# PSUM banks around the values of a forgetting attention: scores' banks for the values, sums' banks for the first projections

## The chip, the cores and the metric

The kernel runs on one core of one Trainium2 chip. The metric is device time in microseconds for one execution; lower is better.

## The reference

One layer of a streaming encoder, for 512 tokens of 1024 channels in float32. Of its three sub-layers the first matters here: four token mixers work on the same normalized input `h`, and their outputs are merged by gates.

```python
h = _rms_norm(x, norm_mix_pre[l])
(a_q, a_k, a_v, f_q, f_k, f_v, f_g, c_u, s_x, s_b, s_c) = jnp.split(h @ w_in[l], cuts, axis=-1)
...                       # A: differential attention, 4 heads, chunk-causal: softmax - lam * softmax, times a_v
ya = (_rms_norm(ya, diff_norm[l]) * (1.0 - lambda_init)).reshape(B, S, BR_W)

log_f = jax.nn.log_sigmoid(f_g.astype(jnp.float32) + b_fgt[l].astype(jnp.float32))
yf = _forgetting_attention(f_q..., f_k..., f_v..., log_f, t_pos)   # B: 8 heads, causal, bias from cumsum(log_f)
...                       # C: convolution module, D: short gated convolution
proj = jnp.einsum('bsnc,ncd->bsnd', br, w_branch[l])
gates = jax.nn.sigmoid(h @ w_gate[l] + b_gate[l]).reshape(B, S, N_BRANCH, D)
mixed = jnp.sum(gates * proj, axis=2) @ w_out[l]
x = x + _rms_norm(mixed, norm_mix_post[l])
...                       # 2. cross-attention into memory tokens, 3. gated MLP
```

## The kernel before

Every product is made at close to full float32 precision from three passes. An operand is split into a high part (rounded by ScalarE's copy, L155 for results in PSUM, L190 for weights) and a low part (VectorE's difference, L156 and L191), and `mm3` (L232 inside `matmul`) adds high x high, high x low and low x high in one PSUM bank. Weights come in blocks of 512 KB on SyncE's queue into a ring of two raw buffers (`wr`) and are split into rings of four high and four low tiles (`wh`, `wl`); `run_blocks` fetches three blocks ahead of the body that uses them.

**Banks.** PSUM has eight banks of 128 x 512 float32, and the kernel gives them out as four rings of two: `mm` (projections and gates), `av` (the sums of values weighted by attention), `sc` (scores) and `tr` (transposes). A tile of a ring waits until the tile two before it has been read. `bank()` without a tag takes `mm` and `av` in turn while `turn_of.shared` is set, and `mm` alone otherwise; `share(flag)` sets this.

**Background tasks.** Attention heads and the convolution's normalization are Python generators in a queue `bg`. Each `yield` names a cost and a wait. `bg.tick()` between the matmul blocks steps the first two tasks of the queue as far as their waits and a credit allow; `bg.drain(name)` steps all tasks of that name to their end. So the generators fix the order in which instructions are written. The order in which each engine runs them is laid down by the framework when the kernel is built: it places an instruction once it takes its inputs and buffers to be ready, the one written first ahead of others. So TensorE runs some of the values' matmuls ahead of pieces of a head that were written earlier. On the chip each engine keeps to its order.

**The stretch around the change,** in the order in which it is written (`mixer_jobs`):

- `v_jobs`: values of differential attention, four token tiles in four banks taken in turn (`av`, `mm`, `av`, `mm`), split into tile `v`.
- `share(False)`, then for each differential head h its query and key (`qk_jobs`: 24 matmuls each, `body_q` leaves the bank by L806 and L807, `body_k` by L815 to L817), and 0, 2, 4 and 6 blocks of gate 2 behind heads 0 to 3. `then(qk)` puts the head's task into the queue.
- `a_task`: steps 0 to 3 each do the scores of one query tile (two `sc` banks, left by VectorE at L877) and a softmax that ends at L887. Steps 1 to 4 transpose the tile before (`tr` bank, `pth` and `ptl`). Steps 3 and 5 do the two halves of the values into one `av` bank, which L892 copies to `head_ck`. Then the head is turned from channels to tokens and back: VectorE transpose (L672), a store to DRAM and four loads on GpSimd's queue (L682, L686), a norm (L898 to L903), VectorE transpose (L678), store and loads again, and L911 with a split into `y["a"]`.
- `drain("a")`, then `vf_jobs`: values of the forgetting attention and its forget gates' inputs, 520 columns in two groups (256 and 264), so two banks a token tile. Token tiles 0 and 1 run over the four weight blocks as they come; then, from the same four blocks, which stay held, tiles 2 and 3. One bank of each token tile is an `mm` and one an `av` bank. `done(t)` splits a token tile into the values tile, which shares the buffer `v` with the differential heads' values. `forget_gates` then makes the cumulative log-forget rows, which go to DRAM (`crows`) on GpSimd's queue.
- `kv_blocks(0)`: query and key of the first pair of forgetting heads, then gate 0 and the other pairs. `f_task` loads rows of `crows` into tiles `ck`, which share their two buffers with `head_ck`.

Of the kernel before, what the change touches and what calls it, by code (L numbers as in the profile page):

```python
# [18 lines left out]
F32R = mybir.dt.float32r  # L19
# [6 lines left out]
P = 128  # L26
S = 512
D = 1024
NT = S // P
# [17 lines left out]
class Background:  # L47
# [26 lines left out]
            while self.credit > 0 and task in self.queue and task[2] <= self.clock:  # L74
                self.credit -= self.step(task)

    def drain(self, name):
        while any(t[0] == name for t in self.queue):
            for task in [t for t in self.queue if t[0] == name][:self.width]:
                self.step(task)  # L80

# [2 lines left out]
def hybrid_layer(ctx: ExitStack, tc: tile.TileContext, a: dict, out: bass.AP):  # L84
# [705 lines left out]

    query_ends = {}

    def qk_jobs(cq, ck, j, then):


        st = {}
        rows = (slice(0, HD), slice(HD, P))

        def body_q(hi, lo):
            qk = st["qk"] = m1p.tile([P, 6, S], F32R, tag="qk", name="qk", bufs=2)  # L800
            for c, r in enumerate(rows):
                G.memset(qk[rows[1 - c], 4 + c].bitcast(F32), 0.0)
            ps = bank()
            channel_major(ps, (hi, lo), ht)
            for c, r in enumerate(rows):
                A.copy(qk[r, c], ps[r])  # L806
                low = V.tensor_tensor(qk[rows[1 - c], c], ps[r], qk[r, c].bitcast(F32), ALU.subtract)  # L807
            query_ends[cq, j] = low.ins

        def body_k(hi, lo):  # L810
            qk = st["qk"]
            ps = bank()
            channel_major(ps, (hi, lo), ht)
            for c, r in enumerate(rows):
                A.copy(qk[r, 2 + c], ps[r])  # L815
                A.copy(qk[rows[1 - c], 2 + c], ps[r])
                V.tensor_tensor(qk[r, 4 + c], ps[r], qk[r, 2 + c].bitcast(F32), ALU.subtract)  # L817
            then(qk)

        yield *cols(w_in, cq + j * P), body_q  # L820
        yield *cols(w_in, ck + j * P), body_k
# [31 lines left out]
    def head_tile(tag):  # L853
        return m1p.tile([P, S], F32, tag=tag, name=f"head_{tag}", bufs=2)

    def a_task(h, qk, v):
        es, pt, av = {}, None, None
        for step in range(6):
            if step in (3, 5):
                if av is None:  # L860
                    av = bank("av")
                vh, vl = (x[:, :, h * P:(h + 1) * P] for x in v[0])
                values(av, lambda kt: ((vh[:, kt], 0), (vh[:, kt], 1), (vl[:, kt], 0)), pt, step // 2 - 1)
            cost = 0.0
            if 1 <= step <= 4:
                if step in (1, 3):
                    pt = pt_tiles()
                to_keys_major(es.pop(step - 1)[:, 0], step, pt[0], pt[1], (step - 1) % 2)
                cost += 0.1 + 0.15 * step
            if step < 4:  # L870
                qt, w = step, (step + 1) * P
                e = es[qt] = e4()
                st = m1p.tile([P, 8], F32, tag="st8", name="st8", bufs=4)
                for c in range(2):
                    ps = bank("sc")
                    scores(ps, qk, c, qt * P, w)
                    V.tensor_tensor_reduce(e[:, c, :w], ps[:, :w], mask_a[:, S - w:], scale=1.0,  # L877
                                           scalar=-3.0e38, op0=ALU.add, op1=ALU.max,
                                           accum_out=st[:, c:c + 1])
                V.tensor_scalar(st[:, 2:4], st[:, 0:2], -HD ** -0.5, None, ALU.mult)  # L880
                for c in range(2):
                    A.activation(e[:, c, :w], e[:, c, :w], AF.Exp, bias=st[:, 2 + c:3 + c],
                                 scale=HD ** -0.5, accum_out=st[:, 4 + c:5 + c])
                V.reciprocal(st[:, 6:8], st[:, 4:6])
                V.tensor_scalar(st[:, 7:8], st[:, 7:8], lam, None, ALU.mult)
                A.activation(e[:, 1, :w], e[:, 1, :w], AF.Copy, scale=st[:, 7:8])
                V.scalar_tensor_tensor(e[:, 0, :w], e[:, 0, :w], st[:, 6:7], e[:, 1, :w], ALU.mult,  # L887
                                       ALU.subtract)
                cost += 0.6 + 0.0035 * w
            if step == 5:  # L890
                o = head_tile("ck")
                A.copy(o, av)  # L892
            yield cost, 3.5

        sq = head_tile("fbias")
        x = head_tile("ck")
        yield from turn(x, o, NT, sq, f"head_tok{h}")
        A.activation(sq, x, AF.Square, scale=1.0 / math.sqrt(P))  # L898
        ms = m1p.tile([P, NT], F32, tag="ms4", name="ms4", bufs=2)
        V.tensor_reduce(ms, sq.rearrange("p (a t c) -> p t a c", a=4, t=NT), AX.XY, ALU.add)  # L900
        r = rstd_of(m1p, [ms], NT)
        x4 = x.rearrange("p (a t c) -> p a t c", a=4, t=NT)
        V.tensor_tensor(x4, x4, r.unsqueeze(1).unsqueeze(3).to_broadcast([P, 4, NT, 32]), ALU.mult)  # L903
        yield 1.5, 1.0
        o = head_tile("ck")
        sq = head_tile("fbias")
        yield from turn(o, x, NT, sq, f"head_chan{h}", True)
        if "a" not in y:
            y["a"] = (y8b(), y8b())
        z = head_tile("fbias")  # L910
        A.activation(z.rearrange("p (t b c) -> p t b c", t=NT, b=4), o.rearrange("p (b t c) -> p t b c", b=4, t=NT),  # L911
                     AF.Identity, scale=half["dn"])
        split(z, y["a"][0][:, h], y["a"][1][:, h])
        yield 0.6, 0.0
# [5 lines left out]
    def vf_jobs(dst):  # L920
# [20 lines left out]
        for kb in range(4):  # L941
            def body(hi, lo, kb=kb):
                held.append((hi, lo))
                if kb == 0:
                    dst.append(m1p.tile([P, NT, 8, 2, HD], F32R, tag="v", name="v"))
                    dst.append(small["fz_raw"].rearrange("p (t h) -> p t h", t=NT))
                    ps.update({(t, g): bank(("mm", "av")[g]) for t in range(2) for g in range(2)})
                products(kb, (0, 1))
                if kb < 3:
                    return  # L950
                done(0)
                done(1)
                bg.tick()
                ps.update({(t, g): bank(("mm", "av")[g]) for t in range(2, 4) for g in range(2)})
                for b in range(4):
                    products(b, (2, 3))
                    bg.tick()
# [150 lines left out]
        return None, None, f  # L1108

    def kv_blocks(p):  # L1110
        return qk_jobs(O_FQ, O_FK, p, lambda qk: bg.add(f_task(p, qk, vf), "f"))

    def mixer_jobs():
        yield from c_jobs()
# [17 lines left out]
            yield then(lambda f=f, q=q: f(q))  # L1132
            yield then(lambda q=q: out_sums.store(q))
        yield from vj
        yield share(False)
        gc = gate_blocks(2, "c")
        for h, n in enumerate((0, 2, 4, 6)):
            yield from qk_jobs(O_AQ, O_AK, h, lambda qk, h=h: bg.add(a_task(h, qk, va), "a"))
            if n:
                yield then(lambda: bg.drain("conv"))  # L1140
            for _ in range(n):
                yield next(gc)
        yield then(lambda: bg.drain("a"))
        yield from vf_jobs(vf)
        yield from kv_blocks(0)
        ga = gate_blocks(0, "a")
        for p in range(1, 4):
# [650 lines left out]
```

## Time and profile before

| | |
|---|---|
| device time, 3 runs | 1064.8, 1064.8, 1069.71 us (median 1064.8) |
| the profiled execution | 1065.52 us, of which its span is 1063.4 us |
| granted TensorE clock, mean | 0.996 |
| busy: TensorE, weight loads | 1044.1 us, 886.6 us |
| busy: VectorE, ScalarE, GpSimd | 806.0 us, 501.1 us, 183.2 us |
| DMA | 163.08 MB, mean 153 GB/s |

In rows of a timeline stand start, duration (us), engine, line, operation, output<-inputs, shapes; in brackets how long the engine was idle before and who ended that. Line numbers are those of the kernel before. In rows of waits stand engine, tile and line, who was waited for, the total in us, how often, and the longest. PE is TensorE, PEld its weight loads, DVE VectorE, ACT ScalarE, POOL GpSimd.

### The profile page before, as it was taken

What the parts mean: (1) busy time and instruction counts of PE and PEld (TensorE: products, weight loads), DVE (VectorE), ACT (ScalarE), POOL (GpSimd) and SP (SyncE); (2) the same over time, 40 slices, a digit from 0 to 9 for tenths busy, and PEclk for the clock granted to TensorE, in tenths of its full rate; (3) what the DMA queues carried; (4) which work ended last, traced back from release to release, by engine and by line L of the source; (5) the groups of instructions that cost most, each with busy time, mean ns of one, the idle gap of its engine ahead of it and who ended that gap; (6) DMA issues with size and microseconds to landing.
All of it is one profiled execution on the core that took longest, in us unless ns stands there. A gap on an engine that the chain in (4) does not pass through costs nothing.

```text
span 1063.4 us, 14555 instructions
## 1 busy us (share of the span) xinstructions
PE 1044.1 (98%) x5295; PEld 886.6 (83%) x5295; DVE 806.0 (76%) x1280; ACT 501.1 (47%) x823; POOL 183.2 (17%) x309
## 2 busy tenths in 40 slices
PE   9999999989999899999999999999999999999995
PEld 8888888878888888888888899998888888888884
DVE  6899997667666467766577798777778778777785
ACT  5322222277564365655443565654333333355661
POOL 4000001200221324322011031121112111111001
PEclk9999999999999999999999999999999999999998
DMA  8854334732443343322358734235676676626652
GB/s 268 291 161 103 103 98 151 196 91 79 124 116 101 98 139 101 99 80 80 119 158 243 252 119 120 79 100 179 198 238 220 216 239 207 206 80 210 205 190 80
DMA packets 165373, 163.08 MB, mean 153 GB/s; under 512 B 6527, under 2 KB 136172, under 8 KB 165045
## 3 DMA queue, kind: packets, MB, share of 16 engines
q1 hardware_dynamic: 152995, 119.91, 37.9%
q0 software_dynamic: 5824, 19.03, 5.9%
q10 hardware_dynamic: 6482, 23.21, 5.7%
q8 instruction: 42, 0.69, 0.3%
q14 instruction: 30, 0.25, 0.1%
HBM read 139.03 MB, written 23.09 MB: 152 GB/s over the span
## 4 chain that ended last, share of the span: by engine, by line
PE 88%; DVE 4%; DMA 3%; issue 2%; ACT 2%; POOL 1%; POOLq 0%; DVEq 0%; ACTq 0%
PE ps_mm L232 48%; PE ps_av L232 27%; PE ps_sc L232 6%; PE ps_tr L232 3%; PE ps_tr L236 2%; DMA dw<-sums 1%; DVE wl L191 1%; DMA xn<-conv_chan 1%; DMA xn<-conv_tok 1%; PE ps_mm L442 1%; DVE wl L1591 1%; PE ps_av L442 1%; PE ps_mm L384 0%; ACT wh L190 0%; DMA wr<-in_w_in 0%
## 5 line engine op out<-in xcount | busy, mean ns | idle before, releaser
L190 ACT CAST wh<-wr 128x1024 fp32r<-128x1024 f32 (+1 forms) x142 | 148.8, 1050 | 266.6 <-PE ps_mm L232 173.6
L232 PE MATMUL ps_mm<-hth,wh 128*128 128x512 f32 (+1 forms) x616 | 230.7, 381 | 4.5 <-DVE qk L807 2.7
L191 DVE TENSOR_TENSOR wl<-wr,wh 128x1024 fp32r<-128x1024 f32 (+1 forms) x142 | 177.8, 1253 | 74.9 <-ACT wh L190 74.7
L232 PE MATMUL ps_mm<-htl,wh 128*128 128x512 f32 (+1 forms) x616 | 230.2, 380 | 0.7 <-DVE htl L156 0.7
L232 PE MATMUL ps_mm<-hth,wl 128*128 128x512 f32 (+1 forms) x616 | 230.1, 380 | 0.0
L232 PEld LDWEIGHTS ps_mm<-hth,wh 128*128 128x128 f32 x616 | 114.1, 188 | 26.6 <-issue 3.1
L232 PEld LDWEIGHTS ps_mm<-htl,wh 128*128 128x128 f32 x616 | 114.1, 188 | 21.5 <-DVE htl L156 0.9
L232 PEld LDWEIGHTS ps_mm<-hth,wl 128*128 128x128 f32 x616 | 113.9, 188 | 21.2
L232 PE MATMUL ps_av<-htl,wh 128*128 128x512 f32 (+1 forms) x328 | 122.5, 373 | 0.0
L232 PE MATMUL ps_av<-hth,wh 128*128 128x512 f32 (+1 forms) x328 | 122.4, 373 | 0.0
L232 PE MATMUL ps_av<-hth,wl 128*128 128x512 f32 (+1 forms) x328 | 122.3, 373 | 0.0
L664 DVE SCALAR_TENSOR_TENSOR y<-y,par,y 128x482 f32<-128x482 f32 (+29 forms) x120 | 82.7, 726 | 0.1
L232 PEld LDWEIGHTS ps_av<-hth,wl 128*128 128x128 f32 x328 | 61.6, 188 | 11.0
L232 PEld LDWEIGHTS ps_av<-hth,wh 128*128 128x128 f32 x328 | 61.6, 188 | 10.9
L232 PEld LDWEIGHTS ps_av<-htl,wh 128*128 128x128 f32 x328 | 61.6, 188 | 10.7
L1591 DVE TENSOR_TENSOR wl<-dw,wh 128x1024 fp32r<-128x1024 f32 x32 | 40.2, 1260 | 12.7 <-ACT wh L1590 12.5
L1590 ACT CAST wh<-dw 128x1024 fp32r<-128x1024 f32 x32 | 33.4, 1051 | 22.4 <-PE ps_mm L232 7.4
L1040 POOL TENSOR_SCALAR fbias<-ck,cq 128x128 f32<-128x128 f32 (+3 forms) x32 | 27.6, 870 | 67.9 <-DVE st L1047 63.5
L1539 ACT ACTIVATE th<-c 128x512 f32<-128x512 f32 x22 | 13.9, 632 | 47.7 <-DVE c L594 47.7
L155 ACT CAST pth<-ps_tr 128x512 fp32r<-128x512 f32 (+3 forms) x56 | 23.4, 448 | 24.7 <-PE ps_tr L236 24.5
L594 DVE SCALAR_TENSOR_TENSOR c<-ps_mm,par,c 128x510 f32<-128x510 f32 (+1 forms) x44 | 32.7, 744 | 0.7
L156 DVE TENSOR_TENSOR ptl<-ps_tr,pth 128x512 fp32r<-128x512 f32 (+3 forms) x56 | 27.7, 513 | 7.3 <-ACT pth L155 7.0
(481 smaller groups left out, 2129.7 us busy)
## 6 DMA issues: line engine op xcount, KB each, us to landing
wr<-in_w_up SPq DMA_DIRECT2D x44, 512.0 KB
wr<-in_w_in SPq DMA_DIRECT2D x38, 512.0 KB
wr<-in_w_gate SPq DMA_DIRECT2D x32, 512.0 KB
wp<-in_w_down ACTq DMA_DIRECT2D x22, 512.0 KB
sums<-wp ACTq DMA_DIRECT2D x22, 512.0 KB
dw<-sums SPq DMA_DIRECT2D x44, 256.0 KB
wr<-in_w_branch SPq DMA_DIRECT2D x16, 512.0 KB
wide<-in_w_out SPq DMA_DIRECT2D x12, 512.0 KB
```

What stands on the lines that cost most here:

```text
L155: A.copy(hi, ps)
L156: V.tensor_tensor(lo, ps, hi.bitcast(F32), ALU.subtract)
L190: order(A.copy(hi, raw[:, :n]))
L191: low.tensor_tensor(lo, raw[:, :n], hi.bitcast(F32), ALU.subtract)
L232: PE.matmul(ps, lhs, rhs, start=start, stop=stop)
L236: PE.transpose(ps, x, ident[:n, :n])
L442: keep(PE.matmul(banks[c][:, :S // 2], w[p == 1][:, k, c * P:(c + 1) * P], ht[p == 2][:, i * 4 + k, :S // 2], start=(i, p, k) == (0, 0, 0) ...
L594: ins = V.scalar_tensor_tensor(dst[:, s:], src[:, :S - s], w(k), dst[:, s:], ALU.mult, ALU.add)
L664: ins = V.scalar_tensor_tensor(dst[:, s:], src[:, :S - s], pc("conv_dw", k * 4 + j), dst[:, s:], ALU.mult, ALU.add)
L1040: G.tensor_scalar(bias[:, :w], ck[j][:, :w], -1.0, cq[:, qt, head:head + 1], ALU.mult, ALU.add)
L1590: A.copy(hi, x)
L1591: V.tensor_tensor(lo, x, hi.bitcast(F32), ALU.subtract)
```

## The change

- `vf_jobs` takes `mm` and `sc` banks instead of `mm` and `av`.
- The first pair of forgetting heads (`kv_blocks(0)`) projects its query and key into `av` banks.
- `share(False)` stands behind the first differential head's query and key, which so take an `av` and an `mm` bank.
- The last differential head gets a name of its own, `a3`. `drain("a")` ends the other heads; `a3` is drained only up to its last scores (step 3) ahead of `vf_jobs`. Its transposes may follow at a tick between the values' blocks. The rest up to the copy of its sums is drained in the last block, between the products of token tiles 0 and 1 and their splits, and the turns through DRAM behind `vf_jobs`.
- The values tile is taken after that drain, not at the first block.

```diff
-    def drain(self, name):
-        while any(t[0] == name for t in self.queue):
+    def drain(self, name, done=lambda: False):
+        while not done() and any(t[0] == name for t in self.queue):
             for task in [t for t in self.queue if t[0] == name][:self.width]:
                 self.step(task)
...
-    def qk_jobs(cq, ck, j, then):
+    def qk_jobs(cq, ck, j, then, tag=None):
...
-            ps = bank()
+            ps = bank(tag)
             channel_major(ps, (hi, lo), ht)
...
+    heads_at = {}
...
             if step < 4:
+                heads_at[h] = step
                 qt, w = step, (step + 1) * P
...
                 A.copy(o, av)
+                heads_at[h] = "values"
             yield cost, 3.5
...
                 if kb == 0:
-                    dst.append(m1p.tile([P, NT, 8, 2, HD], F32R, tag="v", name="v"))
-                    dst.append(small["fz_raw"].rearrange("p (t h) -> p t h", t=NT))
-                    ps.update({(t, g): bank(("mm", "av")[g]) for t in range(2) for g in range(2)})
+                    ps.update({(t, g): bank(("mm", "sc")[g]) for t in range(2) for g in range(2)})
                 products(kb, (0, 1))
                 if kb < 3:
                     return
+                bg.drain("a3", lambda: heads_at[3] == "values")
+                dst.append(m1p.tile([P, NT, 8, 2, HD], F32R, tag="v", name="v"))
+                dst.append(small["fz_raw"].rearrange("p (t h) -> p t h", t=NT))
                 done(0)
                 done(1)
                 bg.tick()
-                ps.update({(t, g): bank(("mm", "av")[g]) for t in range(2, 4) for g in range(2)})
+                ps.update({(t, g): bank(("mm", "sc")[g]) for t in range(2, 4) for g in range(2)})
...
-        return qk_jobs(O_FQ, O_FK, p, lambda qk: bg.add(f_task(p, qk, vf), "f"))
+        return qk_jobs(O_FQ, O_FK, p, lambda qk: bg.add(f_task(p, qk, vf), "f"), None if p else "av")
...
         yield from vj
-        yield share(False)
         gc = gate_blocks(2, "c")
         for h, n in enumerate((0, 2, 4, 6)):
-            yield from qk_jobs(O_AQ, O_AK, h, lambda qk, h=h: bg.add(a_task(h, qk, va), "a"))
+            yield from qk_jobs(O_AQ, O_AK, h, lambda qk, h=h: bg.add(a_task(h, qk, va), "a3" if h == 3 else "a"))
+            if n == 0:
+                yield share(False)
...
         yield then(lambda: bg.drain("a"))
+        yield then(lambda: bg.drain("a3", lambda: heads_at.get(3) in (3, "values")))
         yield from vf_jobs(vf)
+        yield then(lambda: bg.drain("a3"))
         yield from kv_blocks(0)
```

More of the change, by code (lines that the diff above doesn't have):

```diff
@@ L811, in body_k @@
             qk = st["qk"]
-            ps = bank()
+            ps = bank(tag)
             channel_major(ps, (hi, lo), ht)
```

## The prediction

> **What bounds the kernel.** I read the page first: busy times, then the chain that ended last. After that came TensorE's own waits in the stretch that the change touches (205 to 375 us), and the timelines of TensorE, VectorE, ScalarE and GpSimd around each of them.
>
> ```profile
> span 1063.4 us, 14555 instructions
> ...
> PE 1044.1 (98%) x5295; PEld 886.6 (83%) x5295; DVE 806.0 (76%) x1280; ACT 501.1 (47%) x823; POOL 183.2 (17%) x309
> ...
> PE 88%; DVE 4%; DMA 3%; issue 2%; ACT 2%; POOL 1%; POOLq 0%; DVEq 0%; ACTq 0%
> ```
>
> TensorE is busy for 98% of the span and carries 88% of the last chain. Only 1063.4 - 1044.1 = 19.3 us of it is idle, so a change that leaves the matmuls as they are can win only idle time back. The waits in the touched stretch:
>
> ```profile
> PE ps_mm L232 <- DVE qk L807: 2.7, 1, 2.7
> PE ps_mm L232 <- DVE v L156: 1.6, 1, 1.6
> PE ps_av L232 <- ACT head_ck L892: 0.7, 1, 0.7
> PE ps_av L232 <- ACT pth L155: 0.7, 1, 0.7
> PE ps_av L232 <- DVE ptl L156: 0.3, 1, 0.3
> ```
>
> These five are three places, and all that the change can win. **A** (2.7) is the second differential head's query projection, waiting for the first head's query to leave its bank. **B** (0.7 + 0.3 + 0.7) is the last head's end. **C** (1.6) is the first forgetting pair, waiting for a bank that the values still hold. The timeline has them as 2.70, 0.67 + 0.34 + 0.68 = 1.69 and 1.60, together 5.99 us, or 0.56%. A measurement of this kernel can tell about 0.5% (5.3 us) from no change.
>
> **Place A: the first head's projections take the alternating banks.** On the edit: `share(False)` now stands behind the first head's query and key. The timelines of TensorE and VectorE:
>
> ```profile
> 209.90 0.39 PE L232 MATMUL ps_mm<-hth,wh 128*128 128x512 f32 x1
> ...
> 220.55 0.39 PE L232 MATMUL ps_mm<-hth,wl 128*128 128x512 f32 x1
> 223.64 0.47 PE L232 MATMUL ps_mm<-hth,wh 128*128 128x512 f32 x1 [2.70 <-DVE qk L807]
> ...
> 228.94 0.22 PE L232 MATMUL ps_sc<-qk 128*128 128x128 f32 x1
> ```
> ```profile
> 205.74 1.22 DVE L191 TENSOR_TENSOR wl<-wr,wh 128x1024 fp32r<-128x1024 f32 x1 [4.21 <-ACT wh L190]
> ...
> 210.71 0.69 DVE L156 TENSOR_TENSOR v<-ps_mm,v 128x512 fp32r<-128x512 f32 x1 [0.67 <-ACT v L155]
> ...
> 222.80 0.69 DVE L807 TENSOR_TENSOR qk<-ps_mm,qk 64x512 fp32r<-64x512 f32 x1
> ...
> 226.71 0.69 DVE L817 TENSOR_TENSOR qk<-ps_mm,qk 64x512 fp32r<-64x512 f32 x1 [0.65 <-ACT qk L816]
> ```
>
> The 48 matmuls from 209.90 to 220.55 are the first head's query and key, 47 steps of 0.2266 us. Today both lie in the two `mm` banks, so the next query waits for L807, which ends at 222.80 + 0.69 = 223.49; TensorE starts 0.15 later. After the change the first query lies in an `av` bank, the key in one `mm` bank, and the second query takes the other, free since the attention's values left it at 210.71 + 0.69. Its weights were there at 206.96 (the first VectorE row). It starts at 220.55 + 0.23 = 220.78.
>
> But the first head's scores stand ahead of the 24th matmul of that query, and they need the key's L817, which ends at 227.40 and hangs on no bank. TensorE would now reach them at 220.78 + 23 x 0.2266 = 225.99 and go on at 227.40 + 0.15 = 227.55. Counted as the 2.70 is (from the end of the matmul before, 226.15), 1.40 us of idle time stays. The second key's bank, the first key's old one, comes free with the same L817. So A wins 1.30, with bounds: 2.70 if the key leaves earlier, 0.9 if the scores are placed a few matmuls sooner.
>
> **Place B: the last head's end between the values' blocks.** Today tokens 0 and 1 have two `mm` banks and one free `av` bank; the other `av` bank is the last head's own, so 24 of their 96 matmuls wait for the head:
>
> ```profile
> 351.87 0.60 PE L236 MATMUL ps_tr<-ident,e 128*128 128x128 f32 x4
> 353.15 0.38 PE L232 MATMUL ps_av<-pth,v 128*128 128x256 f32 x1 [0.67 <-ACT pth L155]
> 353.87 0.38 PE L232 MATMUL ps_av<-ptl,v 128*128 128x256 f32 x1 [0.34 <-DVE ptl L156]
> ...
> 355.09 0.27 PE L232 MATMUL ps_av<-pth,v 128*128 128x128 f32 x1
> 356.04 0.39 PE L232 MATMUL ps_av<-wh,hth 128*128 128x264 f32 x1 [0.68 <-ACT head_ck L892]
> ...
> 358.94 0.28 PE L232 MATMUL ps_av<-wh,htl 128*128 128x264 f32 x1
> 359.06 0.28 PE L232 MATMUL ps_mm<-wh,hth 128*128 128x256 f32 x1
> ```
> ```profile
> 355.40 0.59 ACT L892 COPY head_ck<-ps_av 128x512 f32<-128x512 f32 x1 [2.31 <-PE ps_av L232]
> 355.88 0.38 ACT L155 CAST v<-ps_mm 128x256 fp32r<-128x256 f32 x1
> ```
> ```profile
> 344.62 0.68 DVE L877 CUSTOM_DVE_ANT_0 e<-ps_sc,mask_a 128x512 f32<-128x512 f32 x1
> ...
> 348.93 0.75 DVE L887 SCALAR_TENSOR_TENSOR e<-e,st 128x512 f32<-128x512 f32 x1
> ...
> 356.02 0.71 DVE L672 STREAM_TRANSPOSE head_fbias<-head_ck 128x512 f32<-128x512 f32 x1 [2.20 <-ACT head_ck L892]
> 356.66 0.67 DVE L678 STREAM_TRANSPOSE head_fbias<-head_ck 128x512 f32<-128x512 f32 x1
> 357.25 0.39 DVE L156 TENSOR_TENSOR v<-ps_mm,v 128x256 fp32r<-128x256 f32 x1
> ```
>
> With the scores' banks, the second of which is free at 344.62 + 0.68 = 345.30, all 96 matmuls can run before the head's values. The 24 (356.04 to 358.94, then 0.12: 3.0 us) fill the 0.67 + 0.34 and end the 0.68. That takes one condition: the four transposes must still come after about 72 of the matmuls, as today. Their input was ready at 348.93 + 0.75 = 349.68, yet TensorE ran them at 351.87, when nothing else was left, so the order laid down in advance has them late.
>
> The 24 are also what today covers the next step, and that cover goes. The values tile shares its space with the heads' values, so no token can leave its bank before the head's last matmul, at 355.09 + 0.27 = 355.36. From there today: copy, cast at 355.88, two transposes, first low part done at 357.25 + 0.39 = 357.64, all unseen behind the 24. Afterwards TensorE has nothing else, as the next weights wait for the four blocks' own slots. The delay from the head's last matmul to token 2, with the 0.15 of place A, would be 355.88 + 0.38 + 0.39 + 0.15 - 355.36 = 1.44 with no transpose in front; 356.66 + 0.39 + 0.15 - 355.36 = 1.84 with one; 357.64 + 0.15 - 355.36 = 2.43 with both. I take one: the last head's own transpose is ready when the copy ends, while the other belongs to an older head and should be through by then. B is then 1.84 against 1.69, a loss of 0.15. Until the `sc` banks come free, the 48 matmuls of the `mm` banks can run (48 x 0.12 = 5.8 us).
>
> **Place C: the first pair's projections in the `av` banks.**
>
> ```profile
> 370.44 0.28 PE L232 MATMUL ps_av<-wh,htl 128*128 128x264 f32 x1
> 372.32 0.50 PE L232 MATMUL ps_mm<-hth,wh 128*128 128x512 f32 x1 [1.60 <-DVE v L156]
> ```
> ```profile
> 364.55 1.22 DVE L191 TENSOR_TENSOR wl<-wr,wh 128x1024 fp32r<-128x1024 f32 x1 [4.39 <-ACT wh L190]
> ```
>
> Both `av` banks are long free by 370.44, and the query's weights are split at 365.77. The 1.60 goes whole. What is late next: the forget gates start from the last token's split, which does not move, so TensorE arrives 1.6 us earlier at the first pair's transposes. The rows that say if it then waits:
>
> ```profile
> 397.83 0.48 DVE L1056 TENSOR_SCALAR e<-e,st 128x128 f32<-128x128 f32 x2
> ```
> ```profile
> 399.99 0.38 PE L236 MATMUL ps_tr<-ident,e 128*128 128x128 f32 x2
> ```
>
> Their input is done at 398.31, 1.68 us ahead; 0.08 is left, so nothing is lost, barely. `drain` itself issues nothing.
>
> **Sum.** Idle before 5.99, after 1.40 + 1.84 + 0 = 3.24: 2.75 us won. Behind this stretch TensorE's longest wait is this:
>
> ```profile
> PE ps_mm L232 <- DVE htl L156: 0.7, 1, 0.7
> ```
>
> So what is won reaches the end. The profiled execution took 1065.52 us (span 1063.4 and 2.1 around it), 0.7 above the median of 1064.8. It would come to 1062.8, and the median to 1062.0.
>
> **Rivals.** *All three waits go* (A 2.70, B 1.69, C 1.60): 1058.8. That needs the key's low parts sooner and other work for TensorE after the head's last matmul. I see neither in the rows; the order of ScalarE and VectorE could change, though. The Trainium skill (Perfetto Trace Analysis, Matmuls) says that independent matmul groups should rotate through different PSUM banks so that the evacuation of one overlaps the next group's matmuls; by that rule more banks alone end all three waits. The trace agrees at C and differs at A, where the scores wait for data and not for a bank.
>
> *The head's end comes after all 96.* If the transposes are placed behind the last of them, 0.67 + 0.34 return, and with both VectorE transposes in front B is 1.01 + 2.43 = 3.44. The sum is 5.99 - (1.40 + 3.44) = 1.15 won: 1063.7. For it speaks how late today's order has the transposes; against it, that 24 matmuls are 3.0 us more.
>
> *Slower: the head's way through DRAM is put behind the values.* The rest of the last head (two round trips through DRAM on GpSimd's queue) now stands in the program behind the values and the forget gates, whose `crows` store is on the same queue. The first pair's `ck` loads need its buffers.
>
> ```profile
> 373.85 0.15 DVE L939 COPY fz_raw<-ps_av 128x8 f32<-128x8 f32 x1
> ```
> ```profile
> 381.86 0.72 ACT L911 ACTIVATE head_fbias<-head_ck,s_dn 128x512 f32<-128x512 f32 x1
> ```
> ```profile
> 390.25 1.17 POOL L1008 DMA_DIRECT2D ck<-crows  x2 [2.68 <-DMA crows<-e]
> ```
>
> Today the buffers are free at 382.58, 7.67 before the loads. If L672 starts only when the last token has left at 374.00 (356.02 today), it is 17.98 late, the loads are 17.98 - 7.67 = 10.31 late, and TensorE waits 10.31 - 1.68 + 1.60 = 10.23 at the first pair: 1062.0 + 10.2 = 1072.2. It makes the kernel slower from a delay of about 10.5 us on (a wait of 2.75), and slower by over 0.5% from 15.8 on. Against it: the transpose is ready at once, and VectorE stands idle then, as it did for 2.20 us before L672.
>
> ```profile
> 200.00:230.00 30.00, 27.30 (x123) 22.40 (x122) 17.18 (x25) 18.80 (x28) 3.41 (x7) 1.00 0.62 171
> ```
>
> With a wait of 2.70 in it, this stretch kept a granted clock of 1.00. The Trainium skill (TensorE: Matmul & The Clock Gate, What's actually happening) has the clock halved after an idle window of about 3.4 us, until another window is busy; no run here shows that, and by an estimate from that page it would add 1.7 us to this rival alone.
>
> **Numbers.** Forecast 0.50, all waits gone 0.14, the head behind all 96 0.24, the DRAM way late 0.12. The range starts at the first rival, 1058.8, rounded to 1058.5. Its upper end is the second with one more wait of the largest size seen (2.70) in an order that I cannot see: 1063.7 + 2.7, rounded to 1066.5. That leaves out the slow rival's 0.12. Faster by over 0.5% (below 1059.5) is the first rival alone, 0.14; slower (above 1070.1) the third, 0.12; the rest, 0.74, lies within.
>
> **What would show it.** In TensorE's waits after: none on L807; about 1.4 in front of the first head's scores or the second key, on L817; no wait on `pth` or `ptl`; one of 1.4 to 2.4 ahead of token 2 on `v` L156; none ahead of the first pair's query. L672's second start should be within 1 us of the head's copy, and `ck` should be loaded no later against TensorE's position than now. I am wrong in kind if TensorE waits at the first pair's transposes for more than 1 us, or if a wait of over 1 us shows outside 205 to 400 us.

## The result, and the profile after

The changed kernel takes 1062.18 us (median of 13 runs, 1059.72 to 1066.17). The kernel before took 1069.07 us in the 13 runs beside them (1064.8 to 1071.66). The ratio is 0.9945, with a 95% interval of 0.9928 to 0.9962: 5.9 us less, between 4.1 and 7.7 (the two medians lie 6.9 apart). So the absolute time was foretold (1062.0), and the difference was not (2.75). That the time itself agrees is luck: the 1064.8 to which the forecast was tied was the lowest of these 13 runs of the kernel before, 4.3 below their median, and the gain was set 4.1 below the difference of the medians.

The profiled execution after took 1062.18 us itself; its span, its busy times and TensorE's waits of 0.3 us or more:

```profile
span 1060.4 us, 14559 instructions
...
PE 1043.6 (98%) x5295; PEld 887.2 (84%) x5295; DVE 804.6 (76%) x1280; ACT 502.4 (47%) x823; POOL 180.1 (17%) x309
...
PE 91%; DMA 3%; issue 2%; DVE 1%; ACT 1%; POOL 1%; POOLq 0%; DVEq 0%; ACTq 0%
```
```profile
PE ps_mm L232 <- DVE v L156: 1.4, 1, 1.4
PE ps_mm L384 <- DVE e L335: 1.3, 1, 1.3
PE ps_mm L232 <- DVE qk L817: 1.3, 1, 1.3
PE ps_sc L232 <- ACT qk L816: 1.1, 2, 0.8
PE ps_sc L232 <- DVE qk L817: 1.0, 2, 0.5
```

The 1.3 on L384 stands at the kernel's start and was there before. The 0.7 on `htl` L156 and another 0.4 on `htl`, far behind the changed stretch, were in the profile before and are not in this one. The rest are the three places and one new wait. Line numbers behind about L850 have moved by 3 to 5: L892 is L895, L939 is L943, L1047 is L1052.

**Place A.** TensorE's timeline, and behind it the rows of ScalarE and VectorE that release it:

```profile
225.79 0.39 PE L232 MATMUL ps_mm<-hth,wl 128*128 128x512 f32 x1
226.42 0.33 PE L232 MATMUL ps_sc<-qk 128*128 128x128 f32 x1 [0.24 <-ACT qk L816]
227.30 0.30 PE L232 MATMUL ps_sc<-qk 128*128 128x128 f32 x1 [0.55 <-DVE qk L817]
228.41 0.33 PE L232 MATMUL ps_sc<-qk 128*128 128x128 f32 x1 [0.82 <-ACT qk L816]
229.23 0.30 PE L232 MATMUL ps_sc<-qk 128*128 128x128 f32 x1 [0.49 <-DVE qk L817]
```
```profile
214.74 0.82 ACT L733 ACTIVATE e<-xn,par 128x512 f32<-128x512 f32 x1 [3.31 <-DMA xn<-conv_chan]
...
220.99 0.56 ACT L806 CAST qk<-ps_av 64x512 fp32r<-64x512 f32 x1
```
```profile
228.39 0.69 DVE L817 TENSOR_TENSOR qk<-ps_mm,qk 64x512 fp32r<-64x512 f32 x1 [0.64 <-ACT qk L816]
```

The bank wait on L807 is gone. The scores now wait 0.24 + 0.55 + 0.82 + 0.49 = 2.10 us for the key, whose second L817 ends at 229.08. The ScalarE rows show why so late: it stood idle for 3.31 us for the load `xn<-conv_chan`, and the convolution's normalization, some 9 us of ScalarE in all (eight activations of 0.8, four casts of 0.6), stands partly in its queue ahead of the head's copies. In the profile before, that load ended ScalarE's idle time 1.68 us sooner:

```profile
213.06 0.81 ACT L733 ACTIVATE e<-xn,par 128x512 f32<-128x512 f32 x1 [1.43 <-DMA xn<-conv_chan]
```

**Place B.** TensorE, ScalarE and VectorE around the last head's end:

```profile
352.47 0.60 PE L236 MATMUL ps_tr<-ident,e 128*128 128x128 f32 x4
...
356.25 0.27 PE L232 MATMUL ps_av<-pth,v 128*128 128x128 f32 x1
...
357.94 0.38 PE L232 MATMUL ps_mm<-wh,hth 128*128 128x256 f32 x1 [1.41 <-DVE v L156]
```
```profile
356.56 0.58 ACT L895 COPY head_ck<-ps_av 128x512 f32<-128x512 f32 x1 [2.87 <-PE ps_av L232]
357.04 0.38 ACT L155 CAST v<-ps_mm 128x256 fp32r<-128x256 f32 x1
```
```profile
349.39 0.70 DVE L678 STREAM_TRANSPOSE head_fbias<-head_ck 128x512 f32<-128x512 f32 x1
...
357.45 0.43 DVE L156 TENSOR_TENSOR v<-ps_mm,v 128x256 fp32r<-128x256 f32 x1 [3.04 <-ACT v L155]
...
358.94 0.70 DVE L672 STREAM_TRANSPOSE head_fbias<-head_ck 128x512 f32<-128x512 f32 x1
```

No wait on `pth` or `ptl` is left; between the head's last matmul and token 2 lie copy, cast and one low part, and no transpose: 1.41 us.

**Place C, and what came behind it.** The first pair's query starts with no wait at 369.53 (372.32 before). Some 30 us later stands the new wait; TensorE's rows, then VectorE's:

```profile
369.53 0.40 PE L232 MATMUL ps_av<-hth,wh 128*128 128x512 f32 x1
...
400.22 0.47 PE L232 MATMUL ps_mm<-hth,wh 128*128 128x512 f32 x1 [1.29 <-DVE qk L817]
```
```profile
395.18 0.29 DVE L1052 CUSTOM_DVE_ANT_0 e<-ps_sc,fbias 128x128 f32<-128x128 f32 x1 [3.09 <-POOL fbias L1047]
...
397.24 0.29 DVE L1052 CUSTOM_DVE_ANT_0 e<-ps_sc,fbias 128x128 f32<-128x128 f32 x1 [0.63 <-POOL fbias L1047]
...
397.46 0.68 DVE L817 TENSOR_TENSOR qk<-ps_mm,qk 64x512 fp32r<-64x512 f32 x1
...
399.38 0.69 DVE L817 TENSOR_TENSOR qk<-ps_mm,qk 64x512 fp32r<-64x512 f32 x1 [1.17 <-ACT qk L816]
```
```profile
390.33 1.17 POOL L1013 DMA_DIRECT2D ck<-crows  x2 [1.83 <-ACT qk L806]
```

VectorE is held at the first pair's rows (L1052) by GpSimd's `fbias`, which needs the `ck` loads (the last row is GpSimd's). These go out at 390.33, as before (390.25), while TensorE is 2.8 us further. The second pair's key leaves its bank by the two L817 behind those rows, and a matmul of the gate waits for that bank.

In the three places and the new wait TensorE waits 2.10 + 1.41 + 1.29 = 4.80 us, against 5.99: only 1.2 of the 3.0 us between the two spans. The two `htl` waits are 1.1 more and TensorE's busy time 0.5.

### The profile page after: what moved, and what is told of

Read it like the earlier page. It is cut to its first block, busy times and chain, and to the rows that moved or that the text cites. A ratio compares the mean times of both kernels' runs of the same rounds, so it can differ in the third digit from the quotient of the medians.

```text
span 1060.4 us, 14559 instructions
## 1 busy us (share of the span) xinstructions
PE 1043.6 (98%) x5295; PEld 887.2 (84%) x5295; DVE 804.6 (76%) x1280; ACT 502.4 (47%) x823; POOL 180.1 (17%) x309
## 4 chain that ended last, share of the span: by engine, by line
PE 91%; DMA 3%; issue 2%; DVE 1%; ACT 1%; POOL 1%; POOLq 0%; DVEq 0%; ACTq 0%
PE ps_mm L232 47%; PE ps_av L232 28%; PE ps_sc L232 8%; PE ps_tr L232 4%; PE ps_tr L236 2%; DMA xn<-conv_chan 1%; DMA xn<-conv_tok 1%; PE ps_mm L442 1%; PE ps_av L442 1%; PE ps_mm L384 0%; ACT wh L190 0%; DMA wr<-in_w_in 0%; DMA ck<-crows 0%; DVE wl L191 0%; DMA head_chan<-head_fbias 0%
## 5 line engine op out<-in xcount | busy, mean ns | idle before, releaser
L232 PE MATMUL ps_mm<-hth,wh 128*128 128x512 f32 (+1 forms) x592 | 220.9, 380 | 1.5 <-DVE qk L817 1.3
L232 PE MATMUL ps_mm<-hth,wl 128*128 128x512 f32 (+1 forms) x592 | 220.8, 380 | 0.0
L232 PE MATMUL ps_mm<-htl,wh 128*128 128x512 f32 (+1 forms) x592 | 220.5, 379 | 0.0
L232 PE MATMUL ps_av<-htl,wh 128*128 128x512 f32 (+1 forms) x352 | 131.8, 375 | 0.0
L232 PE MATMUL ps_av<-hth,wh 128*128 128x512 f32 (+1 forms) x352 | 131.8, 375 | 0.0
L232 PE MATMUL ps_av<-hth,wl 128*128 128x512 f32 (+1 forms) x352 | 131.7, 374 | 0.0
L232 PEld LDWEIGHTS ps_mm<-hth,wl 128*128 128x128 f32 x592 | 109.5, 188 | 20.1
L232 PEld LDWEIGHTS ps_mm<-htl,wh 128*128 128x128 f32 x592 | 109.6, 188 | 19.9
L232 PEld LDWEIGHTS ps_av<-hth,wl 128*128 128x128 f32 x352 | 66.2, 188 | 11.9
L232 PEld LDWEIGHTS ps_av<-htl,wh 128*128 128x128 f32 x352 | 66.1, 188 | 11.8
L156 DVE TENSOR_TENSOR ptl<-ps_tr,pth 128x512 fp32r<-128x512 f32 (+3 forms) x56 | 27.8, 511 | 8.5 <-ACT pth L155 8.3
```

The source lines that it names most:

```text
L156: V.tensor_tensor(lo, ps, hi.bitcast(F32), ALU.subtract)
L232: PE.matmul(ps, lhs, rhs, start=start, stop=stop)
```

## The experiments

Theory 1 is the prediction's: the gain is made at TensorE's waits through the banks. Theory 2 looks for it outside these waits: elsewhere in the kernel, or in a longer span with the same idle time. Theory 3 is that place A is the lateness of `xn<-conv_chan`, handed on by ScalarE's queue.

**The kernel before, once more.** No edit; a second profile.

> The kernel before, unchanged, as a measure of what a repeat does. Theory 1 (the change wins at three waits of TensorE and nowhere else): TensorE waits 2.7, 1.7 and 1.6 us at places A, B and C again, and any longer time of a repeat comes from a wait that hangs on a transfer. Theory 2 (the kernel before has a slower mode somewhere else, which the change happens to avoid): a repeat of 1068 us or more shows 3 to 6 us of TensorE idle time outside 205 to 400 us, or a longer span with the same idle time.

1068.71 us, ratio 1.001 (0.999 to 1.0029). Its profiled execution, at 1072.63 us one of its longest, is not like the first one (1065.52). TensorE's timeline at place A, ScalarE's, and the busy times of all engines in stretches (the number ahead of the last two is the granted clock):

```profile
227.98 0.76 PE L232 MATMUL ps_mm<-hth,wh 128*128 128x512 f32 x1 [6.66 <-DVE qk L807]
```
```profile
217.41 0.82 ACT L733 ACTIVATE e<-xn,par 128x512 f32<-128x512 f32 x1 [5.39 <-DMA xn<-conv_chan]
```
```profile
226.00:228.00 2.00, 0.02 (x1) 0.05 (x1) 1.94 (x4) 1.93 (x4) 1.04 (x2) 0.61 0.87 245
228.00:230.00 2.00, 2.00 (x5) 1.61 (x6) 1.97 (x3) 1.79 (x4) 0.00 (x0) 0.50 0.00 0
230.00:232.00 2.00, 2.00 (x7) 1.52 (x6) 1.10 (x2) 1.01 (x2) 0.00 (x0) 0.50 0.77 213
232.00:234.00 2.00, 2.00 (x8) 1.59 (x7) 0.00 (x0) 0.00 (x0) 0.00 (x0) 0.68 0.17 49
362.00:366.00 4.00, 3.33 (x16) 3.19 (x16) 2.35 (x6) 1.41 (x4) 1.16 (x2) 0.62 0.23 85
```

The load came 4.35 us later, place A grew by 3.96, and the clock fell behind A and behind B. TensorE's busy time was 1047.3 us instead of 1044.1. So the span is 7.0 us longer by 4.0 of waiting at A and 3.2 of slower matmuls. Theory 1 had expected 2.7 us at A and longer times from waits alone; the second part is what theory 2 asked about, busy time, though it stands right behind the waits. Place A is no fixed 2.7 us, and a wait can cost more than its length.

**The share alone.** Before, with only the first differential head's projections taken in turn from both rings:

```diff
-        yield share(False)
         gc = gate_blocks(2, "c")
...
+            if n == 0:
+                yield share(False)
```

> Only place A: share(False) behind the first differential head's query and key, all else as before. Theory 1: the 2.7 us in front of the second query goes, 1.4 to 2.1 us appear at the first head's scores, B (1.7) and C (1.6) stay as before; the time falls by 0.6 to 1.3 us. Theory 2: nearly the whole gain (about 6 us in the medians) comes with this edit, or nearly none of it and B and C are as before.

1063.78 us, ratio 0.9971 (0.9951 to 0.9992). The profile has 4.51 us at A, all at the scores, with the load at 217.18; B and C stand as before (0.7 + 0.7 + 0.3 and 1.8). The places are as theory 1 had them, but the gain of 3.1 us by the ratio is more than its 0.6 to 1.3.

**All but the share.** After, with `share(False)` back ahead of the first head:

> The change without place A: share(False) back in front of the first head. Theory 1: A is 2.7 us again, B 1.4, C 0 and then 1.3 us behind the second pair's key, as in the kernel after; the time lies 0.6 to 1.3 us above the kernel after, 1.2 us or so below the kernel before. Theory 2: the time equals the kernel after within 0.5 us, or that of before.

1066.28 us, ratio 0.9984 (0.9968 to 0.9999). The wait on L807 is back with 4.22 us (load at 214.32), `v` L156 is 1.4, and the new wait on L817 near 400 us is 2.1. So the share and the rest each bring part of the gain (the rest only barely clear of none), and 0.9971 x 0.9984 = 0.9955 is nearly the whole. Here too the sizes are off: the time lies 4 us above the kernel after, where 0.6 to 1.3 was expected. The new wait belongs to the rest: with the share alone it is not there.

**The first pair in the scores' banks.** Before, with `bank("sc")` for the first pair's query and key:

> Only place C, and with other free banks: the kernel before, with the first forgetting pair's query and key in the scores' banks (idle then) instead of mm banks. Theory 1: any free bank does; the 1.6 us ahead of the first pair's query goes, A (2.7) and B (1.7) stay, and about 1.3 us come back behind the second pair's key, where VectorE's queue stands behind the first pair's bias; net 0.3 us less, not to be told from none in time. Rival: the 1.6 us stays, since the query waits for its weights or for VectorE and not for the bank.

1068.62 us, ratio 1.0011 (0.9992 to 1.003): nothing won, and the wait stayed, as the rival had it, but not for its reason (late weights or VectorE). TensorE's timeline:

```profile
371.33 0.28 PE L232 MATMUL ps_av<-wh,htl 128*128 128x264 f32 x1
373.26 0.50 PE L232 MATMUL ps_mm<-hth,wh 128*128 128x512 f32 x1 [1.65 <-DVE v L156]
...
384.05 0.60 PE L236 MATMUL ps_sc<-ident,fz 128*8 128x128 f32 x4
384.41 0.48 PE L232 MATMUL ps_sc<-hth,wh 128*128 128x512 f32 x1
```

The first two projections that TensorE comes to stand in `mm` still. Those in `sc` follow at 384.41, right behind the forget gates' transposes, which take a tile of the same ring and are written ahead of them. That ring order caused this was read from code and rows, not tried. If so, an empty bank is of use only where its ring has no tile that is written earlier and starts later; the `av` ring has none here. A wait of 0.79 us on L817 came up at 403 us in this kernel as well.

**The head's end asked for in one piece.** After, with `a3` drained to its end ahead of the values:

```diff
-        yield then(lambda: bg.drain("a3", lambda: heads_at.get(3) in (3, "values")))
+        yield then(lambda: bg.drain("a3"))
```

> The kernel after with one part undone: the last differential head is drained whole ahead of the values' blocks, as before; the banks stay those of the kernel after. Theory 1: where the head's end is written decides nothing, since the order on each engine goes by readiness; B is 1.4 us with the same rows on TensorE, and the time is that of the kernel after (1062.2, within the spread of its runs). Rival (standing between the blocks is what covers the transposes): the 0.7 and 0.3 us in front of the head's values come back, B is 2.4 us or more.

1063.89 us, ratio 0.9957 (0.9936 to 0.9978). Between 195 and 428 us TensorE, ScalarE and VectorE run the same instructions in the same order as after. So where the head's end is written decides nothing here, as theory 1 had it, and the waits on the transposes' copies do not come back as the rival had it: what is left of the change at B are the banks and the values tile taken later. The run also stands as a second measurement of the order after, with 2.41 us at A (load at 214.68), 1.4 at B and 1.9 near 400 us.

**The normalization behind the first head's key.** After, and also before, with the activations L733 and L734 held back on ScalarE:

```diff
+        while (O_AQ, 0) not in key_ends:
+            yield 0.0, 0.5
...
+            with tc.issue_after(key_ends[O_AQ, 0][0]):
                 A.activation(one, turned_y[:, j], AF.Identity, ...)
                 A.activation(two, turned_y[:, j], AF.Tanh, ...)
```

> The kernel after, with the convolution's last ScalarE activations (which wait for the load of xn from DRAM, 212.3 to 217.4 us in the runs so far) put on ScalarE's queue behind the first differential head's key. Theory 3 (place A is that load, passed on by ScalarE's queue to L806 and L815, in front of which those activations stand; the bank only decides how much of it TensorE sees): the waits at the first head's scores go to under 0.3 us, the granted clock stays at 1.00 there, the spread of the runs falls from 6.5 us to 3 or less, and the median falls by 2 to 4 us against 1062.2. Theory 1 (banks alone): the same waits of about 2 us at the scores, since no bank changes.

> The kernel before with the same edit and no bank changed. Theory 3: the wait of 2.5 to 6.7 us in front of the second query goes without any new bank, and with it the halved clock behind it; the median falls from 1068.6 by 4 to 6 us and the spread to 3 us or less; B (1.7) and C (1.6 to 1.8) stay. Theory 1: the wait stays at 2.5 us or more, since the query still needs the bank of the first one.

1072.68 us after (ratio 1.0035, 1.0018 to 1.0052) and 1073.32 before (1.0049, 1.0029 to 1.0068). Place A's waits went in both, with and without the new banks, as theory 3 says. Both medians were expected to fall, though, and rose by about 4 us against the kernel before: the work has to be done somewhere. TensorE's and ScalarE's rows of the first of the two (its L811, L820 and L821 are L806, L815 and L816):

```profile
240.80 0.44 PE L232 MATMUL ps_sc<-qk 128*128 128x128 f32 x1 [6.08 <-ACT y L158]
```
```profile
238.00 0.62 ACT L158 ACTIVATE y<-e 128x512 fp32r<-128x512 f32 x1
238.52 0.57 ACT L811 CAST qk<-ps_mm 64x512 fp32r<-64x512 f32 x1
238.98 0.58 ACT L820 CAST qk<-ps_mm 64x512 fp32r<-64x512 f32 x1
...
240.18 0.63 ACT L158 ACTIVATE y<-e 128x512 fp32r<-128x512 f32 x1
```

The normalization now stands in front of the second head's copies, and the second head's scores wait 6.08 us in each of the two profiles. The clock fell to 0.50 with it. Either kernel's runs lie within 4.0 us of each other, against 9.2 for the kernel before beside them. That fits a load that is off the path, but it does not show it alone: all 19 runs have a mean clock of 0.990 to 0.992, where those of the kernel before go from 0.990 to 0.997, so a clock that falls in every run narrows them too.

**Half of the normalization behind the key.** The same edit for the third and fourth pair of activations alone.

> The kernel after, with only the third and fourth of the four conv-normalisation activation pairs (L733, L734) held back behind the first head's key copies on ScalarE; the first two start when the load xn<-conv_chan lands, as before. Theory 3 (place A is the load's lateness passed on by ScalarE's queue): the first two pairs are about 1.5 us each plus a 0.6 us split copy, the other half of about 4.5 us is out of the way, so the 2.1 to 2.4 us of waits at the first head's scores fall below 1 us where the load lands at about 214.7 us; the half put later stands in front of the second head's evictions with half of the 6.08 us, about 1.5 to 3 us. Sum within 1 us of the kernel after, ratio 0.993 to 0.998, and the median's range narrower than the kernel after's. Rival (the wait at the second head's scores comes from the second head's tile, which takes the normalisation's buffer, and not from ScalarE's time): the wait there stays at 5 us or more whatever is moved, ratio 1.002 to 1.005.

1062.73 us, ratio 0.9954 (0.9934 to 0.9973). Place A is 0.82 + 0.50 = 1.32 us with the load at 215.24, less than after's 2.10, and the second head's scores wait for nothing, where 1.5 to 3 us were expected. The rival's 5 us or more is not there, so the 6.08 was ScalarE's time and not a buffer. The expectation of a narrower range failed (1059.45 to 1065.92), and the time is the kernel after's. In this profile the clock took back what A gave:

```profile
228.00:230.00 2.00, 2.00 (x7) 1.62 (x8) 1.43 (x6) 2.00 (x3) 0.00 (x0) 0.66 0.23 66
230.00:232.00 2.00, 2.00 (x7) 1.51 (x6) 2.00 (x4) 1.98 (x5) 0.97 (x2) 0.50 0.00 2
232.00:234.00 2.00, 2.00 (x10) 1.66 (x9) 1.90 (x5) 1.95 (x7) 0.06 (x1) 0.98 0.75 261
```

That is about 1.7 us of lost time: (0.34 + 0.50 + 0.02) x 2. It does not explain the median, since the mean clock over all runs is the kernel after's (0.9959, there 0.9958); 0.8 us less at A is too little to be told in time.

**The head's end further ahead.** After, with the last block's products of tokens 0 and 1 put behind the head's transposes and behind its values:

```diff
+                bg.drain("a3", lambda: heads_at[3] == "values")
+                for t, step in enumerate((4, 5)):
+                    with tc.issue_after(head_ends[3, step]):
+                        products(kb, (t,))
```

> The kernel after with an order forced on TensorE: the last block's products of token tile 0 come behind the last head's transposes, and those of token tile 1 behind the head's values, so that 12 matmuls (1.45 us) stand between the head's values and token tile 2. My step for B (what is left there is the chain copy, cast, low part with nothing on TensorE beside it): the 1.4 us on v goes to under 0.3, and at most 0.3 us shows on ptl; B wins 1.1 us or more, hardly to be told in time. Rival: the 1.4 us only moves, to the head's values (waiting for pth and ptl) or to token tile 2.

1061.63 us, ratio 0.9939 (0.9917 to 0.9961). Place B is gone whole: the head's values now have matmuls behind them that hide copy, cast and low part. The new wait near 400 us is still there (1.0).

**The first pair behind the second key.** After, with the first L1052 rows behind the second pair's key instead of its query:

```diff
-                    with tc.issue_after(query_ends[O_FQ, 1]) if p + step == 0 else ExitStack():
+                    with tc.issue_after(key_ends[O_FQ, 1][1]) if p + step == 0 else ExitStack():
```

> The kernel after, with the first forgetting pair's first VectorE rows (L1052, whose start came 3.09 us after VectorE fell idle, behind the load-bound fbias of L1047) put behind the second pair's key eviction L817 instead of behind its query eviction L807. Theory 1 (the 1.29 us wait of the gate's matmul at 400.22 us is the key's two L817, which stand behind those rows in VectorE's order): the wait on L817 at about 400 us goes, and nothing else opens within 10 us of it, so the profile's waits fall by 1.3 us and the median by about 1 us against the kernel after, ratio 0.993 to 0.995 (the kernel after has 0.9945). Rival (the rows are the later link: the first pair's transposes and with them TensorE's next step come late): a wait of 1 us or more on the first pair's own bank or on e, between 395 and 410 us, takes its place, ratio 0.9945 or above.

1060.95 us, ratio 0.9938 (0.9915 to 0.9961). The new wait is gone, and nothing took its place between 360 and 420 us. VectorE's rows (L818 is L817, L1054 is L1052):

```profile
392.74 0.68 DVE L818 TENSOR_TENSOR qk<-ps_mm,qk 64x512 fp32r<-64x512 f32 x1
394.67 0.69 DVE L818 TENSOR_TENSOR qk<-ps_mm,qk 64x512 fp32r<-64x512 f32 x1 [1.25 <-ACT qk L817]
395.39 0.29 DVE L1054 CUSTOM_DVE_ANT_0 e<-ps_sc,fbias 128x128 f32<-128x128 f32 x1
```

**Both, and all three.** The last two edits together, and with the half normalization added:

> The kernel after with two of its three waits taken away: the values' second half of the first two tokens put around the last head's end (as in the run of the values earlier, 1061.63 us, ratio 0.9939) and the first pair's rows behind the second pair's key. Theory 1: no wait on v L156 and none on L817 near 400 us, what is left on TensorE is place A's 2.1 to 2.4 us and the 1.3 us near the start, ratio 0.992 to 0.994. Rival (each wait that goes comes back later on the same chain, as at the gate): a new wait of 1 us or more between 360 and 410 us, ratio 0.9945 or above.

> All three edits at once on the kernel after: half of the conv normalisation behind the first head's key, the values around the last head's end, the first pair's rows behind the second pair's key. If each place is independent: the ratio is that of the kernel with the last two, plus what the split run differs from the kernel after, 0.990 to 0.996; if the split brings a wait of 2 us or more and a halved clock at the second head's scores (.50 in 2 us slices, as in the run with all of the normalisation moved), 0.996 to 1.000.

1057.35 us, ratio 0.9924 (0.9896 to 0.9952, 7 runs), and 1060.75 us, ratio 0.9933 (0.991 to 0.9955). The first has the lowest median of the study and beats the kernel before. Against the kernel after its point lies 0.2% lower, but the intervals overlap, so that it beats that one is not shown. Its profile, taken in its longest execution (1062.43 us), has neither B nor the new wait, and only A of the three places:

```profile
PE ps_sc L232 <- ACT qk L817: 3.4, 2, 2.6
PE ps_mm L384 <- DVE e L335: 1.3, 1, 1.3
PE ps_sc L232 <- DVE qk L818: 1.1, 2, 0.6
```

A is 4.47 us here, not the 2.1 to 2.4 expected, with the load at 216.94. With all three edits A is 2.78 us at the latest load of all (217.99), B and the new wait are gone, and the second head's scores wait for nothing; in time the half normalization adds nothing that can be told.

**Place A over the profiles whose normalization is where it was,** by the start of its first row behind the load:

| kernel | load there, us | waits at A, us | TensorE busy, us |
|---|---|---|---|
| first head in `mm` alone: first pair in `sc` | 212.31 | 2.50 | 1044.9 |
| same: before | 213.06 | 2.70 | 1044.1 |
| same: all but the share | 214.32 | 4.22 | 1044.0 |
| same: before, once more | 217.41 | 6.66 | 1047.3 |
| first head in both rings: pair behind second key | 213.41 | 0.75 | 1042.6 |
| same: head's end in one piece | 214.68 | 2.41 | 1044.0 |
| same: values earlier | 214.72 | 2.24 | 1043.6 |
| same: after | 214.74 | 2.10 | 1043.6 |
| same: values and pair | 216.94 | 4.47 | 1044.0 |
| same: the share alone | 217.18 | 4.51 | 1048.8 |

With the load within 0.4 us of each other (before and the pair behind the key; all but the share and the head in one piece; before once more and the share alone), the share is worth 1.95, 1.81 and 2.15 us. Each us by which the load is late costs 0.8 us in the upper half ((6.66 - 2.50) / 5.10) and 1.1 in the lower (3.72 / 3.53).

**The clock of every run.** Each run's span and mean granted clock are on record, not only the profiled one's. Span x (1 - clock) is an estimate of the time that the clock took. It holds a part that costs nothing: at the kernel's end, where TensorE has no more work, the clock is low too, for 2.6 to 4.3 us by this measure in the profiles. Means over the runs:

| kernel | runs | span, us | span x (1 - clock), us |
|---|---|---|---|
| before, beside the experiments | 89 | 1066.0 | 6.8 |
| the share alone | 12 | 1062.7 | 5.3 |
| all but the share | 12 | 1064.5 | 6.2 |
| after | 13 | 1060.6 | 4.4 |
| head's end in one piece (the order after) | 12 | 1062.0 | 4.9 |
| after, normalization behind the key | 12 | 1070.7 | 9.4 |
| before, normalization behind the key | 7 | 1071.1 | 8.7 |

Before and after differ by 5.4 us in span and by 2.4 in the last column; the head's end in one piece and the 24 runs of before beside it differ by 4.4 and 2.2. So roughly 2 us of the gain is matmuls that run at the full clock more often, and the rest, 2 to 3 us, is idle time. In all 14 profiles, each stretch of 2 us with a clock under 0.93 ahead of that end lies within a wait at A, B, C, the second head's scores or the new wait, or within 2 us behind one, with the half clock going on from there. So the clock's share hangs on the same waits; which of them sets it off is told below as far as it is known.

## Why the prediction was right or wrong

**Place A: mechanism right, size wrong.** The query no longer waits and the key's L817 is what is left, as foretold. The term of 1.40 was mis-sized twice, in opposite ways. First, it was counted as one wait up to the last L817, but the four scores take the key's parts as they come: three of them, 0.33 + 0.30 + 0.33 = 0.96 us of work, run inside it. At the load's time of before that would leave 0.44 us, a win of 2.26; the pairs of the table give 1.8 to 2.2. Second, L817 "hangs on no bank", and the prediction took its 227.40 as fixed. It hangs on the load, which came 1.68 us later in the profile after: 1.40 + 1.68 - 0.96 = 2.12, against the 2.10 in the rows.

**Place B: right but for the transpose.** The transposes came behind 78 matmuls (about 72 foretold), the waits on `pth` and `ptl` went, and token 2 is what is late. The 1.84 rested on one VectorE transpose in front of the low part. There was none: the older head's had run at 349.39, and the last head's own came behind the low parts, 1.8 us after the copy. So the lower bound, 1.44, held with 1.41. The sign "L672 within 1 us of the copy" failed by the same step.

**Place C: right; what was late next, wrong.** The 1.60 went whole. "0.08 is left, so nothing is lost, barely" looked at the first pair's transposes alone. The same late `fbias` also holds VectorE's queue, and in it the second pair's L817: 1.29 us of the 1.60 came back there. The sign of an unchanged `ck` load against TensorE's position failed too (2.8 us later by it). By its own letter the test for "wrong in kind", a wait of over 1 us outside 205 to 400, is met by 0.2 us.

**The sum: the step that it lacked is the clock.** At the load's time of before the corrected terms are 5.99 - (0.44 + 1.41 + 1.29) = 2.85 us, beside the 2.75 foretold: three errors (the gain set 0.96 and 0.43 too low at A and B, 1.29 too high behind C) that nearly cancel, which is luck. Both are under the 4.1 at which the measured gain's interval begins. The step that failed is that "a change that leaves the matmuls as they are can win only idle time back", and that the waits are "all that the change can win". The one profile it was read from was a short execution, with the load early and a full clock from A to C, so that the waits looked free of any cost but their length. The runs' clocks show the rest: the same matmuls took about 2 us less on average after the change, because the clock was low for less of the time. What is left is 2 to 3 us of idle time, about what was foretold. The split is rough: it is worked out from mean clocks of three decimals, the part at the kernel's end differs by up to 1.7 us between profiles, and the kernels of the table did not all run side by side.

**The rivals.** All waits gone (1058.8) did not come about with the change, though the later runs show that two of the three are to be had. The rule behind it, that matmul groups rotate through banks so that evacuation overlaps (the Trainium skill, Perfetto Trace Analysis, Matmuls), is borne out by the 1.8 to 2.2 us of the share; beyond that the scores waited for data, 2.10 us of it. The head's end behind all 96 matmuls was not seen (78), nor the last head's way through DRAM behind the values: L672 starts it at 358.94, with token 2 only begun, and the `ck` loads go out when they did before.

## What to carry to other kernels

A wait that ends on an engine's copy may be another engine's load in disguise: look at what stood ahead of that copy in its in-order queue, and how far that start moves between executions, before taking its length as a constant. When a bank is freed, the next late step is sought in every queue that the late input holds up, not only at its own consumer. A sum of waits from one profile also leaves out the clock: look at the granted clock of other executions behind the same waits. And work moved off one waiting spot in a queue has to be short enough for the next one: moving all of the normalization cost a wait of 6.08 us, moving half of it none there.

## What was not expected of the hardware

The clock fell after waits of very different length, and not after some longer ones. It kept 1.00 behind the 2.70 us of the first profile before and behind the 2.10 of after. It fell to about half for 1.7 us of lost time behind 1.32 us in two pieces (half of the normalization moved), behind 2.50 in one piece (first pair in `sc`: 0.56 and 0.58 in two stretches of 2 us) and behind 2.41 in four (head's end in one piece: 0.57 and 0.58). With the 6.66 it was low from 226 to 234 us, 3.4 us lost, and with the 6.08 from 238 to 249, 5.1 lost: (0.47 + 4 x 0.50 + 0.09) x 2. The Trainium skill (TensorE: Matmul & The Clock Gate, What's actually happening) has the clock halved after an idle window of about 3.4 us, and says that the window runs freely. At half the clock, 1.7, 3.4 and 5.1 us lost are stretches of about once, twice and three times that length; but waits of under 3.4 us set them off here, so the page's figure is no safe floor, and where a wait falls may count beside its length.

The load `xn<-conv_chan` was there between 212.3 and 218.0 us over the twelve profiles that show it, and runs of one kernel lie up to 9.9 us apart (the share alone). What makes that load late was not tried.
